# A scheduler's queue model learns that GpSimd sums delay queued VectorE work, and side work waits for GpSimd's queue

## The chip, the cores and the metric

One core of one Trainium2 chip. The metric is the device time of one launch in microseconds; lower is better. The engines are TensorE (PE, its weight loads PEld), VectorE (DVE), ScalarE (ACT), GpSimd (POOL) and SyncE (SP, which issues the DMAs).

## What is computed

One layer of a hybrid decoder for a prompt of 512 tokens and 8 sample tokens that share all weights. Everything is float32 at the interface. Cut to what matters:

```python
h = rms_norm(x, g); z = h @ w_in                      # (520, 2048) @ (2048, 7168)
y = [ silu(gate_pool) * Pool(u) |                     # trailing means over 2/4/8/16 positions
      silu(gate_dil)  * DilAttn(q, k, v) |            # 3 groups of 4 heads, QK-norm, merged by denominators
      silu(gate_mem)  * MemAttn(q_mem, mem) ]         # 4 heads over 256 memory tokens, QK-norm
x = x + y @ w_out                                     # (520, 1536) @ (1536, 2048)
```

The memory keys and values come from `rms_norm(mem) @ w_mem_kv` (2048 x 1024). The sample tokens attend to cached windows, and the shifted caches are outputs too.

## The kernel before

All activations are kept transposed (128 channels on the partitions, 520 tokens along the free axis). Every weight block of 128 x 512 is loaded by a DMA (`wraw`), and split in two float32r parts, `whi` by ScalarE (L167) and `wlo` by VectorE (L177); activations are split as `xh`, `xl` in the same way. A product is then three matmuls (xh·whi, xl·whi, xh·wlo), each over two halves of 260 tokens. The function `emit_split` makes one split and issues the next load; `whi` and `wlo` have 6 buffers each (SPB). I count the splits from 0, in the order in which VectorE makes them: 16 for the first four blocks (0 to 15), 12 for the next three z blocks (16 to 27), then the stage that mixes four z blocks with the eight blocks of `w_mem` (the memory stage, splits 28 to 75: a memory block's split feeds 12 matmuls of 256 columns, a z block's 24 of 260), then the other z blocks, then the 16 output blocks.

Between the matmuls of this main stream, side tasks run as Python generators: the norm of each q and k (`norm_task`: Square, a sum over partitions on GpSimd by `p_ar` at L210, `rsqrt_steps`, then a product), the sample tokens' scores and values (`sample_scores`, `sample_values`), the attentions and the pool branch (`pool_task`). A task takes one step when it is advanced. What is issued when is decided while the program is built, by the class `Clock`: it keeps an estimated time for each engine (`free`), for TensorE (`pe`) and for each tile (`written`, `used`). The order so made is the program: every engine runs its instructions in that order.

```python
def busy():
    return ck.backlog("dve") > 2.5 or ck.backlog("act") > 2.5
def tick():
    budget = ck.pe + 1.2
    for task in list(tasks):
        if task[0] > ck.pe: continue
        if ck.pe > budget or busy(): break
        if not advance(task): tasks.remove(task)
```

`tick` is called after every six main matmuls. `task[0]` is the estimated time at which the task's last step ends, plus 1 us. `backlog(eng)` is `free[eng] - pe`. `p_ar` calls `Clock.hold(s, e)`: VectorE instructions that the model places in that stretch are put behind it, and if VectorE's queue already reaches beyond `s`, its `free` time is moved by `e - s`. At the end of the z stage the output blocks begin (`need_split`): before the matmuls that read a slot of y (12 slots in the order YORDER, the last one of the pool branch's group 0) the tasks are pushed until that slot is there.

Of the kernel before, what the change touches and what calls it, by code (L numbers as in the profile page):

```python
# [48 lines left out]
class Clock:  # L49
# [5 lines left out]
    def __init__(self):  # L55
        self.pe = 0.0
        self.free = {"act": 0.0, "dve": 0.0, "pool": 0.0, "sp": 0.0, "hbm": 0.0}
        self.last = 0.0
        self.written = {}
        self.used = {}  # L60
        self.held = []

    def after(self, ins, outs):
        t = 0.0
        for a in ins:
            t = max(t, self.written.get(a.tensor.name, 0.0))
        for a in outs:
            t = max(t, self.used.get(a.tensor.name, 0.0))
        return t
# [11 lines left out]
    def use(self, eng, dur, ins, outs, shared=True):  # L81
        if eng == "pe":
            dep = max([self.written.get(a.tensor.name, 0.0) for a in ins])
            self.pe = max(self.pe, dep) + dur
            end = self.pe
            for a in ins:
                n = a.tensor.name
                self.used[n] = max(self.used.get(n, 0.0), end)
            for a in outs:
                n = a.tensor.name  # L90
                self.written[n] = max(self.written.get(n, 0.0), end + self.LAT)
                self.used[n] = max(self.used.get(n, 0.0), end)
            self.last = max(self.last, end + self.LAT)
            return
        start = max(self.free[eng], self.after(ins, outs))
        if eng == "dve" and shared and not any(a.tensor.name.startswith("ps") for a in ins):
            for s, e in self.held:
                if s <= start < e:
                    start = e
        end = start + dur  # L100
        self.free[eng] = end
        self.done(end + self.LAT, ins, outs)

    def hold(self, s, e):

        if s < self.free["dve"]:
            self.free["dve"] += e - s
        self.held = [h for h in self.held if h[1] > self.pe] + [(s, e)]

    def dma(self, nbytes, ins, outs):  # L110
# [17 lines left out]
def trunk(ctx, tc, nc, I, O):  # L128
    ck = Clock()
# [117 lines left out]
        return True  # L247

    def busy():
        return ck.backlog("dve") > 2.5 or ck.backlog("act") > 2.5  # L250

    def tick():
        budget = ck.pe + 1.2
        for task in list(tasks):
            if task[0] > ck.pe:
                continue
            if ck.pe > budget or busy():
                break
            if not advance(task):
                tasks.remove(task)  # L260
# [792 lines left out]
    for g, (w, d) in enumerate(WINS):  # L1053
        a, n, e = D2D[g]
# [290 lines left out]
```

## Time and profile before

| | us |
|---|---|
| median of 3 runs (894.66 to 895.25) | 895.0 |
| the profiled execution | 894.77 |
| its span | 893.0 |
| PE busy | 884.6 (99%) |
| PEld busy | 873.5 |
| DVE busy | 647.2 (72%) |
| ACT busy | 388.4 (43%) |
| POOL busy | 286.8 (32%) |

The granted TensorE clock is 1.00 over the span. 1.8 us of the profiled execution lie outside its span. A busy time is the sum of the instructions' own times; an instruction that is held up while it runs counts as busy for that time too.

### The profile page before, as it was taken

What the parts mean: (1) busy time and instruction counts of PE and PEld (TensorE: products, weight loads), DVE (VectorE), ACT (ScalarE), POOL (GpSimd) and SP (SyncE); (2) the same over time, 40 slices, a digit from 0 to 9 for tenths busy, and PEclk for the clock granted to TensorE, in tenths of its full rate; (3) what the DMA queues carried; (4) which work ended last, traced back from release to release, by engine and by line L of the source; (5) the groups of instructions that cost most, each with busy time, mean ns of one, the idle gap of its engine ahead of it and who ended that gap; (6) DMA issues with size and microseconds to landing.
All of it is one profiled execution on the core that took longest, in us unless ns stands there. A gap on an engine that the chain in (4) does not pass through costs nothing.

```text
span 893.0 us, 18390 instructions
## 1 busy us (share of the span) xinstructions
PE 884.6 (99%) x7226; PEld 873.5 (98%) x7226; DVE 647.2 (72%) x1226; ACT 388.4 (43%) x796; POOL 286.8 (32%) x96
## 2 busy tenths in 40 slices
PE   9999999999999999999999999999999999999998
PEld 8999999999999999999999999999999999999998
DVE  6788899965487869988798886888769679422321
ACT  7665565534436434544335343345433615222220
POOL 0133364613346345533155522363334400000000
PEclk9999999999999999999999999999999999999999
DMA  9535346589977867677878799689887777799421
GB/s 325 196 128 184 129 162 197 172 265 315 332 256 246 277 212 233 240 267 257 302 229 304 221 335 338 216 306 313 287 277 259 285 255 242 261 409 330 145 79 49
DMA packets 84663, 219.57 MB, mean 246 GB/s; under 512 B 10712, under 2 KB 25176, under 8 KB 82392
## 3 DMA queue, kind: packets, MB, share of 16 engines
q1 hardware_dynamic: 84432, 218.13, 71.8%
q8 instruction: 56, 0.92, 0.4%
q14 instruction: 31, 0.25, 0.1%
q10 hardware_dynamic: 144, 0.26, 0.1%
HBM read 200.32 MB, written 106.25 MB: 343 GB/s over the span
## 4 chain that ended last, share of the span: by engine, by line
PE 93%; DVE 4%; issue 1%; DMA 1%; SPq 0%; ACT 0%; DVEq 0%
PE psm L220 81%; PE psb L220 12%; DVE wlo L177 1%; DVE sv L200 1%; PE psb L226 1%; DMA vn<-xT 0%; DVE sq L181 0%; DVE sk L177 0%; DVE tmp L181 0%; DMA o_mem<-vt 0%; DVE vt L177 0%; DVE qk L177 0%; DVE smx L196 0%; DVE tmp L177 0%; SPq L230 0%
## 5 line engine op out<-in xcount | busy, mean ns | idle before, releaser
L220 PE MATMUL psm<-xh,whi 128*128 128x260 f32 x2088 | 431.5, 287 | 1.6 <-ACT whi L167 0.7
L220 PE MATMUL psm<-xh,wlo 128*128 128x260 f32 x2088 | 422.9, 283 | 2.4 <-DVE wlo L177 2.3
L220 PE MATMUL psm<-xl,whi 128*128 128x260 f32 x2088 | 421.9, 283 | 0.0
L220 PEld LDWEIGHTS psm<-xh,whi 128*128 128x128 f32 x2088 | 323.8, 189 | 8.4 <-issue 5.5
L220 PEld LDWEIGHTS psm<-xh,wlo 128*128 128x128 f32 x2088 | 322.6, 188 | 3.2 <-DVE wlo L177 3.2
L220 PEld LDWEIGHTS psm<-xl,whi 128*128 128x128 f32 x2088 | 322.2, 188 | 0.0
L177 DVE TENSOR_TENSOR wlo<-wraw,whi 128x512 fp32r<-128x512 f32 x304 | 248.6, 838 | 47.9 <-ACT whi L167 47.8
L167 ACT ACTIVATE whi<-wraw 128x512 fp32r<-128x512 f32 x304 | 180.0, 621 | 169.2 <-PE psm L220 137.9
L210 POOL PARTITION_ALL_REDUCE sk<-sk x32 | 131.0, 4094 | 175.6 <-DVE sk L177 128.8
L210 POOL PARTITION_ALL_REDUCE sq<-sq x32 | 102.7, 3213 | 128.3 <-ACT sq L167 128.3
L177 DVE TENSOR_TENSOR tmp<-psm,vn 128x260 f32<-128x260 f32 x30 | 11.5, 424 | 89.5 <-PE psm L220 79.3
L167 ACT ACTIVATE sk<-sk,smx 128x256 f32<-128x256 f32 (+1 forms) x64 | 35.4, 553 | 71.0 <-DVE smx L187 37.0
L210 POOL PARTITION_ALL_REDUCE mx<-mx x17 | 46.6, 2739 | 55.0 <-DVE mx L177 55.0
L167 ACT ACTIVATE tmp<-tmp 128x520 f32<-128x520 f32 (+2 forms) x76 | 46.3, 610 | 33.8 <-DVE sq L181 28.7
L167 ACT ACTIVATE sq<-qk 128x520 f32<-128x520 f32 x28 | 17.8, 634 | 71.9 <-DVE qk L177 63.6
L220 PE MATMUL psb<-y,whi 128*128 128x256 f32 x192 | 41.3, 282 | 0.0
L177 DVE TENSOR_TENSOR qk<-psm,rsx 128x260 f32<-128x260 f32 x56 | 21.2, 420 | 22.7 <-PE psm L220 22.7
L220 PE MATMUL psb<-y,wlo 128*128 128x256 f32 x128 | 35.9, 281 | 0.0
L167 ACT ACTIVATE tmp<-sq,eps 128x520 f32<-128x520 f32 (+1 forms) x32 | 22.2, 695 | 28.2 <-POOL sq L210 27.8
L220 PEld LDWEIGHTS psb<-y,whi 128*128 128x128 f32 x192 | 31.6, 188 | 0.0
L200 DVE CUSTOM_DVE_ANT_1 sv<-sv,sk,sy 128x384 f32<-128x384 f32 x32 | 31.1, 1009 | 0.6
L181 DVE SCALAR_TENSOR_TENSOR qk<-qk,gains_r,sq 128x520 f32<-128x520 f32 x28 | 27.7, 989 | 1.0
(131 smaller groups left out, 742.3 us busy)
## 6 DMA issues: line engine op xcount, KB each, us to landing
o_cache<-cache SPq DMA_DIRECT2D x88, 712.0 KB, 7.3
wraw<-w_in SPq DMA_DIRECT2D x208, 256.0 KB, 5.3
o_cache<-cache SPq DMA_DIRECT2D x24, 584.0 KB, 6.3
wraw<-w_out SPq DMA_DIRECT2D x48, 256.0 KB, 4.9
wraw<-w_mem SPq DMA_DIRECT2D x32, 256.0 KB, 3.9
vn<-xT SPq DMA_DIRECT2D x31, 260.0 KB, 5.3
o_zero<-zero SPq DMA_DIRECT2D x6, 1024.0 KB, 7.3
sk<-dks SPq DMA_DIRECT2D x16, 384.0 KB, 5.4
```

The source lines that it names most:

```text
L167: nc.scalar.activation(out=out, in_=in_, func=func, scale=scale, bias=bias, **kw)
L177: nc.vector.tensor_tensor(out=out, in0=in0, in1=in1, op=op)
L181: nc.vector.scalar_tensor_tensor(out=out, in0=in0, scalar=scalar, in1=in1, op0=op0, op1=op1)
L200: nc.vector.tensor_tensor_reduce(out=out, in0=in0, in1=in1, scale=1.0, scalar=init, op0=op0, op1=op1, accum_out=accum)
L210: nc.gpsimd.partition_all_reduce(t, t, P, op)
L220: nc.tensor.matmul(out, lhsT=lhsT, rhs=rhs, start=start, stop=stop)
L226: nc.tensor.transpose(out, in_, ident)
```

## The change

The model's class keeps a list `recent` of the tiles that VectorE's queued instructions write, with their estimated ends. When a sum on GpSimd holds VectorE from `s` to `e`, the tiles in `recent` that end later than `s + 0.7` are now taken to be written and free `e - s` later; before, only the engine's `free` time was moved. And `busy()`, which keeps `tick` from beginning steps of side tasks, is now true as well when GpSimd's estimated queue is more than 1.0 us ahead of TensorE. No instruction is added or removed; their order changes on every engine.

```diff
@@ class Clock
+        self.recent = []
@@ use(): after an instruction of any engine but TensorE
         end = start + dur
         self.free[eng] = end
         self.done(end + self.LAT, ins, outs)
+        if eng == "dve":
+            self.recent = [r for r in self.recent if r[1] > self.pe] + [(a.tensor.name, end) for a in outs]
 
     def hold(self, s, e):
 
         if s < self.free["dve"]:
             self.free["dve"] += e - s
+            late = [(n, t) for n, t in self.recent if t > s + 0.7]
+            self.recent = [r for r in self.recent if r not in late] + [(n, t + e - s) for n, t in late]
+            for n, t in late:
+                self.written[n] = max(self.written[n], t + e - s + self.LAT)
+                self.used[n] = max(self.used[n], t + e - s + self.LAT)
         self.held = [h for h in self.held if h[1] > self.pe] + [(s, e)]
@@ trunk()
     def busy():
-        return ck.backlog("dve") > 2.5 or ck.backlog("act") > 2.5
+        return ck.backlog("dve") > 2.5 or ck.backlog("act") > 2.5 or ck.backlog("pool") > 1.0
```

In the rows that follow, source lines of the change are 8 higher than those of before (L185 is the former L177, L175 the former L167, L228 the former L220).

VectorE in the memory stage, from the `wlo` of split 43 to that of split 46 (`smx`, `sk` are the sample tokens' scores, `tmp`, `sq`, `qk` the end of a norm). Before:

```order
L177 TENSOR_TENSOR wlo_1631<-wraw_1368,whi_1630 128x512
L177 TENSOR_TENSOR wlo_1651<-wraw_1402,whi_1650 128x512
L177 TENSOR_TENSOR wlo_1669<-wraw_1423,whi_1668 128x512
L192 COPY qms_83<-qk_795 128x8
L192 COPY cs_84<-vt_1553 128x8
L177 TENSOR_TENSOR wlo_1707<-wraw_1446,whi_1706 128x512
```

In the change:

```order
L185 TENSOR_TENSOR wlo_1648<-wraw_1368,whi_1647 128x512
L185 TENSOR_TENSOR wlo_1668<-wraw_1409,whi_1667 128x512
L185 TENSOR_TENSOR wlo_1687<-wraw_1428,whi_1686 128x512
L204 TENSOR_REDUCE smx_1698<-sk_984 128x2
L195 TENSOR_SCALAR smx_1698<-smx_1698 128x2
L185 TENSOR_TENSOR sk_1637<-sk_1637,qms_83 128x512
L189 SCALAR_TENSOR_TENSOR tmp_1704<-sq_1594,tmp_1704 128x520
L189 SCALAR_TENSOR_TENSOR sq_1594<-tmp_1704,tmp_1703 128x520
L189 SCALAR_TENSOR_TENSOR qk_995<-qk_995,gains_r_66,sq_1594 128x520
L185 TENSOR_TENSOR wlo_1737<-wraw_1446,whi_1736 128x512
```

Two copies of 8 elements stood between the splits 45 and 46; now a score's maximum, the next score's product and the end of a norm stand there.

ScalarE a little earlier, from the `whi` of split 33 to that of split 35 (`tmp` with `eps`, `tmp`, `tmp` are the three steps of a reciprocal root, `sq` with `qk` the Square of the next norm). Before:

```order
L167 ACTIVATE whi_1364<-wraw_1020 128x512
L167 ACTIVATE sq_1383<-qk_795 128x520
L167 ACTIVATE whi_1398<-wraw_1067 128x512
L167 ACTIVATE whi_1419<-wraw_1105 128x512
L167 ACTIVATE tmp_1435<-sq_1262,eps_67 128x520
L167 ACTIVATE tmp_1434<-tmp_1435 128x520
```

In the change:

```order
L175 ACTIVATE whi_1364<-wraw_1020 128x512
L175 ACTIVATE tmp_1381<-sq_1262,eps_67 128x520
L175 ACTIVATE tmp_1380<-tmp_1381 128x520
L175 ACTIVATE tmp_1381<-tmp_1380 128x520
L175 ACTIVATE sq_1397<-qk_795 128x520
L175 ACTIVATE whi_1405<-wraw_1067 128x512
L175 ACTIVATE whi_1424<-wraw_1105 128x512
```

The reciprocal root's three steps and the Square now stand ahead of the `whi` of splits 34 and 35.

TensorE at the beginning of the output blocks, around the last of the pool branch's four products (`vt`, `kmem`, which here holds `pool_w`); `xh_35` is the slot that this product's result ends in, by VectorE's y, ScalarE's `xh_35` and VectorE's `xl_51`. Before:

```order
L220 MATMUL psb_9939<-vt_9872,kmem_625_3700 128x260
L220 MATMUL psb_9940<-vt_9872,kmem_625_3700 128x260
L220 MATMUL psm_9793<-xh_32_95,whi_9853 128x260 x2
L220 MATMUL psm_9793<-xl_48_111,whi_9853 128x260 x2
L220 MATMUL psm_9793<-xh_32_95,wlo_9854 128x260 x2
L220 MATMUL psm_9793<-xh_33_96,whi_9853 128x260 x2
L220 MATMUL psm_9793<-xl_49_112,whi_9853 128x260 x2
L220 MATMUL psm_9793<-xh_33_96,wlo_9854 128x260 x2
L220 MATMUL psm_9793<-xh_34_97,whi_9853 128x260 x2
L220 MATMUL psm_9793<-xl_50_113,whi_9853 128x260 x2
L220 MATMUL psm_9793<-xh_34_97,wlo_9854 128x260 x2
L220 MATMUL psm_9793<-xh_35_98,whi_9853 128x260 x2
```

In the change:

```order
L228 MATMUL psm_9771<-xh_34_97,wlo_9850 128x260 x2
L228 MATMUL psb_9957<-vt_9909,kmem_629_3691 128x260
L228 MATMUL psb_9958<-vt_9909,kmem_629_3691 128x260
L228 MATMUL psm_9771<-xh_35_98,whi_9849 128x260 x2
L228 MATMUL psm_9771<-xl_51_114,whi_9849 128x260 x2
```

The product stood 18 main matmuls ahead of the first reader of its slot; now it stands directly ahead of it.

## Rows read from the trace of the kernel before

**Rows 1.** The page: busy time of the engines.

```profile
PE 884.6 (99%) x7226; PEld 873.5 (98%) x7226; DVE 647.2 (72%) x1226; ACT 388.4 (43%) x796; POOL 286.8 (32%) x96
```

**Rows 2.** TensorE's waits: who, us in total, times, longest.

```profile
PE psm L220 <- DVE wlo L177: 2.3, 3, 1.2
PE psm L220 <- ACT whi L167: 0.7, 1, 0.7
```

**Rows 3.** Windows: stretch and length, then PE, PEld, DVE, ACT, POOL busy, clock, DMA.

```profile
93.60:121.50 27.90, 26.71 (x225) 26.51 (x223) 24.73 (x37) 16.72 (x33) 14.26 (x4) 1.00 0.40 132
121.50:154.30 32.80, 32.80 (x278) 32.80 (x277) 29.86 (x60) 19.66 (x43) 12.69 (x5) 1.00 0.61 197
154.30:181.00 26.70, 25.70 (x217) 25.49 (x216) 25.16 (x47) 15.89 (x37) 14.51 (x6) 1.00 0.60 188
```

**Rows 4.** Timeline of ACT, 92 to 100 us: start, length, instruction, idle before.

```profile
92.59 0.62 ACT L167 ACTIVATE whi<-wraw 128x512 fp32r<-128x512 f32 x1
...
93.64 1.14 ACT L167 ACTIVATE whi<-wraw 128x512 fp32r<-128x512 f32 x2
...
97.97 1.31 ACT L167 ACTIVATE tmp<-tmp 128x520 f32<-128x520 f32 x2 [2.58 <-DVE mx L181]
```

**Rows 5.** Timeline of DVE, 92 to 100 us.

```profile
92.43 1.89 DVE L177 TENSOR_TENSOR wlo<-wraw,whi 128x512 fp32r<-128x512 f32 x3
...
97.00 0.41 DVE L181 SCALAR_TENSOR_TENSOR tmp<-mx,tmp 128x256 f32<-128x256 f32 x1
97.45 0.43 DVE L181 SCALAR_TENSOR_TENSOR mx<-tmp,tmp 128x256 f32<-128x256 f32 x1
```

**Rows 6.** Timeline of PE: the matmul that reads split 34's wlo first.

```profile
99.02 0.40 PE L220 MATMUL psm<-xh,wlo 128*128 128x260 f32 x2
```

**Rows 7.** Timeline of DVE, 107 to 133 us.

```profile
109.46 0.68 DVE L177 TENSOR_TENSOR sk<-sk,qms 128x512 f32<-128x512 f32 x1
...
111.00 2.40 DVE L181 SCALAR_TENSOR_TENSOR tmp<-sq,tmp 128x520 f32<-128x520 f32 x1
...
114.17 2.65 DVE L181 SCALAR_TENSOR_TENSOR qk<-qk,gains_r,sq 128x520 f32<-128x520 f32 x1
...
120.78 0.68 DVE L177 TENSOR_TENSOR wlo<-wraw,whi 128x512 fp32r<-128x512 f32 x1
121.39 0.15 DVE L206 RECIPROCAL sz<-sz 128x2 f32<-128x2 f32 x1
...
122.36 1.29 DVE L177 TENSOR_TENSOR wlo<-wraw,whi 128x512 fp32r<-128x512 f32 x2
...
124.50 0.68 DVE L196 TENSOR_REDUCE smx<-sk 128x2 f32<-128x512 f32 x1
...
125.29 0.69 DVE L181 SCALAR_TENSOR_TENSOR tmp<-sq,tmp 128x520 f32<-128x520 f32 x1
...
127.43 1.28 DVE L177 TENSOR_TENSOR wlo<-wraw,whi 128x512 fp32r<-128x512 f32 x2
```

**Rows 8.** Timeline of POOL, 92 to 130 us.

```profile
110.24 3.60 POOL L210 PARTITION_ALL_REDUCE sk<-sk  x1 [12.78 <-DVE sk L177]
113.74 3.53 POOL L210 PARTITION_ALL_REDUCE sq<-sq  x1
```

**Rows 9.** Timeline of PE: the first readers of the wlo of splits 43, 46, 50.

```profile
117.48 0.51 PE L220 MATMUL psm<-xh,wlo 128*128 128x260 f32 x2 [1.19 <-DVE wlo L177]
...
123.28 0.40 PE L220 MATMUL psm<-xh,wlo 128*128 128x260 f32 x2
...
131.59 0.28 PE L220 MATMUL psb<-y,wlo 128*128 128x256 f32 x1
```

**Rows 10.** Timeline of PE: the last product of the pool branch.

```profile
760.74 1.04 PE L220 MATMUL psb<-vt,kmem 128*128 128x260 f32 x4
```

**Rows 11.** Timeline of ACT: the slot of y that waits for that product.

```profile
762.34 0.64 ACT L167 ACTIVATE xh<-y 128x520 fp32r<-128x520 f32 x1 [3.60 <-DVE y L181]
```

**Rows 12.** Timeline of DVE: the slot's second part.

```profile
763.01 0.70 DVE L177 TENSOR_TENSOR xl<-y,xh 128x520 fp32r<-128x520 f32 x1 [0.71 <-ACT xh L167]
```

## The prediction

> **What bounds the kernel now.** I read the page first. TensorE is busy for 884.6 of the span's 893.0 us, at the full granted clock [rows 1, 3], and the change adds and removes no matmul. So a better order can give back at most what TensorE loses in waits. TensorE's own waits come next: three waits for a `wlo` make 2.3 us, and one for a `whi`, at the program's first product, 0.7 us [rows 2]. The kernel can thus become at most some 2.3 us faster by a better order, and as much slower as a worse order makes splits late. Third, the windows of the stretch where those waits lie, the memory stage: VectorE is busy for 24.73 of 27.90, 29.86 of 32.80 and 25.16 of 26.70 us there [rows 3]. It has only 3.2, 2.9 and 1.5 us of air in these three pieces, and every `wlo` stands in its queue. In this stage the order on VectorE decides; later VectorE has more air. Last, the program's order before and in the change, at the places shown with the change.
>
> What a sum on GpSimd costs VectorE is in two pairs of rows. The sum of 110.24 found `tmp` begun at 111.00, which took 2.40 us, where the same instruction takes 0.69 us elsewhere: 1.7 us more. The sum of 113.74 found `qk` begun at 114.17, which ended at 116.82, 3.1 us after the sum's begin, where the triple `tmp`, `sq`, `qk` otherwise takes 2.14 us in all (125.29 to 127.43), so that `qk` lost about 1.9 us [rows 7, 8]. An instruction caught in a sum comes free about 2.2 to 2.5 us after the sum's begin. I price a sum that catches VectorE's queue at 1.7 to 1.9 us.
>
> **The change, part by part.**
>
> *The model's new lines themselves* cost nothing at run time: they act while the program is built. All that counts is the order.
>
> *Place 1, splits 34 and 35 on ScalarE.* Before, `whi` of 34 and 35 stood ahead of a reciprocal root; they ran at 93.64, and the root's second step then waited 2.58 us for VectorE's `mx`, harmlessly [rows 4]. In the change the root and a Square stand ahead of them. I walk it: VectorE's three `wlo` end their slots at 94.24 (three of 0.60 from 92.43), `tmp` and `mx` follow (0.41 and 0.43 with 0.04 between), so `mx` is there at 95.1 [rows 5]. ScalarE's two steps then take 1.31 [rows 4], the Square 0.6, `whi` of split 34 another 0.6: 97.6. The Square releases a sum on GpSimd at about 97.1, which catches the `wlo` of split 34 and lets it end at about 99.9 (97.1, 2.2 and 0.6). TensorE wanted it at 99.02 [rows 6]. That is a new wait of 0.9 us.
>
> *Place 2, split 46.* Ahead of its `wlo`, counted from where the orders part, VectorE has in the change one norm triple (2.14), one maximum with its scaling (0.79, 124.50 to 125.29), one score product (0.60) and one set of the sample's values (0.97, 121.39 to 122.36) more than before, and nothing less: 4.5 us [rows 7]. The score product that comes forward releases one sum more, too: with 1.9 it is 6.4 us. Before, that `wlo` ended at 121.46 and TensorE read it at 123.28 [rows 7, 9], a lead of 1.8. If VectorE idles as much as before, TensorE gets there 4.6 us later than before; if all 3.2 us of air of this stretch [rows 3] were filled, 1.4 us later. Place 1 leaves VectorE waiting from about 95.5 to 97.6, some 2.1 us of air that isn't filled, so at most 1.1 us is won: 3.5 to 4.6. I take 4.0. In this number place 1's wait is contained, and also that the old wait of 1.19 us at split 43 [rows 9] goes.
>
> *Place 3, split 50.* From split 49 to 50 a set of values and a triple now stand (0.97 and 2.14) where a maximum and a triple stood (0.79 and 2.14), and a norm's Square ahead on ScalarE makes a sum fall in. Extra 0.2 and 1.9; the lead there is about 1.7: before, the `wlo` ended at 128.1 (127.43 and 0.68) and was read at 131.59, a lead of 3.5 [rows 7, 9], of which the 1.8 of split 46 are used up. That leaves 0.4, and 1.2 if VectorE also waits for buffers that the late TensorE frees late. I take 1.0, bounds 0 and 1.9.
>
> *The rest of the memory stage, splits 51 to 75.* By split 76 the order has one half-width triple more ahead than at place 2, some 1.3 us (its steps take 0.41 and 0.43 [rows 5]). The last two pieces have 2.9 and 1.5 us of air [rows 3], already used by an order that had leads of 2 to 4 us. I price further short waits at 1.5 us together. Below, the old wait late in the stage (2.3 less the 1.19 of split 43 leaves at most 1.1 us [rows 2, 9]) could go without a new one, -1.1; above, two more places like place 2 without air, +4.
>
> *The later z blocks.* TensorE loses hardly anything to a split there before [rows 2], and by split 128 the same instructions stand ahead of it in both orders. I take nothing.
>
> *The first output block.* The last product of the pool branch stands directly ahead of the matmul that reads its result. Before, 18 matmuls of 0.12 us, 2.2 us, lay between. The chain from the product's begin: 760.74 to the end of `xh` at 762.98 and of `xl` at 763.71 [rows 10 to 12], while TensorE has issued the product's four passes about 0.7 us after its begin (1.04 less the last one's flight), at 761.45. With nothing between, TensorE waits 1.5 us for `xh`, does two matmuls (0.24) and waits 0.45 us more for `xl`: 2.0 us. Bounds: 1.5, if other splits of the slot's neighbours aren't in the way, and 2.4, if a `whi` or a `wlo` stands ahead on ScalarE or VectorE. DMA queues: the loads and stores follow the splits and tasks and bring the same bytes; I cost their moves at nothing, since the loads run 10 buffers ahead.
>
> **Sum.** 4.0 + 1.0 + 1.5 + 2.0 = 8.5 us. On the profiled execution's 894.77 (893.0 of span and 1.8 around it) this is 903.3; the median of the runs is 0.2 higher, so **903.5 us**, 0.9% slower. Low ends together: 1.4 + 0 - 1.1 + 1.5 = 1.8, or 896.8. High ends: 4.6 + 1.9 + 4 + 2.4 = 12.9, or 907.9. About 0.2% (1.8 us) is what a measurement of this kernel can tell from no change.
>
> **Rivals.**
>
> *The model is right and the order fits the chip better (faster).* Then the three waits for a `wlo` go without new ones, and nothing is lost at the output blocks: 2.3 us less [rows 2], 892.7. For it: the order before met sums that came later than planned. Against it: place 1 and place 2 can be counted, and the product at the output block stands where it stands. It decides at split 46: if its `wlo` is there by TensorE's need, this is the case. 6%.
>
> *VectorE's air takes most of it.* Place 2 comes to 1.4, places 3 and the rest to 0, the output block to 2.0: 3.2 us, 898.2. For it: in the stretch to 121.5 VectorE did idle 3.2 us. Against it: place 1 puts 2.1 us of idling in the same stretch. 22%, from 897 to 900.
>
> *It stays the same*, because the gains at the old waits (2.3) pay for place 2 at its low end and the output block: 895 to 896. 6%.
>
> *TensorE's clock falls.* The granted clock stayed at 1.00 in every stretch of rows 3, with waits of at most 1.2 us in them; the new wait at split 46 would be some 3 us. If the clock fell to the lower of its two levels, each microsecond of matmuls after it would take two until it rose, and 6 to 8 us of such a stretch give 3 to 4 more: about 907. The Trainium skill ("TensorE: Matmul & The Clock Gate", Part 1, "What's actually happening") says that the throttled clock is the default and that activity releases it; no run here shows what gap ends that. 5%.
>
> **How the numbers follow.** The forecast with its neighbourhood (900 to 907) has 61%, and these four 39%. Slower by over 0.2% are the forecast, the second rival and the last: 0.88. Within 0.2%: 0.06. Faster: 0.06. The range leaves out the faster case, the unchanged one and the last: **897.5 to 907.0**.
>
> **What would show it.** Right: a wait of TensorE for `wlo` of about 1 us near 100 us and one of 3 to 4 us near 127 us, further ones of about 1 us before 185 us, and near 771 us TensorE waiting 1.5 us for `xh` and 0.4 for `xl`; the wait of 1.19 at 117 gone; DVE's busy share of the memory stage nearly the same over a longer stretch. Wrong in the first step: no wait at 100. Wrong in the main step: split 46's `wlo` ahead of TensorE's need, or no extra sum on GpSimd before it. The output block is independent of both: if the whole is slower by only about 2 us, the memory stage was misjudged.

## The result and the profile after

| | before | after |
|---|---|---|
| median, us | 894.97 (894.66 to 895.25) | 905.46 (904.9 to 907.17) |
| span of the profiled execution, us | 893.0 | 905.4 |

The change makes the kernel 1.2% slower: the ratio is 1.0121, with an interval of 1.0109 to 1.0133. The forecast of 903.5 us was 2.0 us too low, and the range (897.5 to 907.0) holds the result. The profiled execution of the changed kernel took 907.17 us, 1.7 us more than its median. Its mean granted clock is 0.998, as in the execution of 905.93 us; the two of 905.0 and 904.9 us have 1.000. So part of what stands in this trace, told below, is not in every execution.

The page of the changed kernel, its busy line. TensorE's busy time has risen by 4.7 us and VectorE's by 21.8 us, with the same number of instructions [rows 1]: both count an instruction as busy while it runs slowly or is held.

```profile
PE 889.3 (98%) x7226; PEld 876.0 (97%) x7226; DVE 669.0 (74%) x1226; ACT 387.0 (43%) x796; POOL 287.2 (32%) x96
```

TensorE's waits in the changed kernel (who, us in total, times, longest). Three waits for a `wlo` with 2.3 us [rows 2] have become eight with 8.3 us, 7.7 us of them in the memory stage; the waits for `xh` and `xl` at the first output block are new.

```profile
PE psm L228 <- DVE wlo L185: 4.4, 5, 1.6
PE psb L228 <- DVE wlo L185: 3.9, 3, 1.7
PE psm L228 <- ACT xh L175: 1.2, 1, 1.2
PE psm L228 <- ACT whi L175: 1.2, 2, 0.7
PE psm L228 <- DVE xl L185: 0.2, 1, 0.2
```

The windows of the memory stage, of the changed kernel (stretch and length, then PE, PEld, DVE, ACT, POOL busy, clock, DMA):

```profile
93.60:128.00 34.40, 30.66 (x253) 30.04 (x252) 30.06 (x46) 18.84 (x41) 17.06 (x5) 1.00 0.43 142
128.00:163.00 35.00, 31.99 (x260) 30.99 (x260) 31.42 (x61) 17.50 (x39) 17.08 (x6) 1.00 0.51 165
163.00:193.00 30.00, 28.28 (x224) 28.02 (x224) 26.12 (x52) 16.87 (x38) 11.70 (x4) 0.94 0.65 209
```

The same three stretches of the kernel before:

```profile
93.60:128.00 34.40, 33.21 (x279) 33.01 (x278) 31.09 (x51) 20.47 (x41) 14.26 (x4) 1.00 0.48 158
128.00:163.00 35.00, 35.00 (x297) 35.00 (x296) 32.09 (x64) 21.22 (x47) 17.12 (x7) 1.00 0.59 191
163.00:193.00 30.00, 29.00 (x242) 28.79 (x241) 26.76 (x49) 16.07 (x37) 13.31 (x5) 1.00 0.61 189
```

By the records TensorE does 26, 37 and 18 matmuls fewer in the three stretches, and VectorE, on which the `wlo` stand, is not fuller but a little emptier: it idles 4.3, 3.6 and 3.9 us where it idled 3.3, 2.9 and 3.2. TensorE waits for VectorE at one split, and VectorE then waits for what comes late: behind split 46 it idles 2.33 us for a `whi` (at 128.44 below).

The timeline of PE in the changed kernel: the matmuls behind the long waits. By the splits that they read they are 34 (99.88), 43 (118.92), 46 (126.17), 50 (136.44), 57 (150.96), the `whi` of 61 (158.81) and 69 (178.00); then the first output block.

```profile
99.88 0.51 PE L228 MATMUL psm<-xh,wlo 128*128 128x260 f32 x2 [0.85 <-DVE wlo L185]
...
118.92 0.51 PE L228 MATMUL psm<-xh,wlo 128*128 128x260 f32 x2 [1.64 <-DVE wlo L185]
...
126.17 0.51 PE L228 MATMUL psm<-xh,wlo 128*128 128x260 f32 x2 [1.24 <-DVE wlo L185]
...
136.44 0.39 PE L228 MATMUL psb<-y,wlo 128*128 128x256 f32 x1 [0.80 <-DVE wlo L185]
...
150.96 0.38 PE L228 MATMUL psb<-y,wlo 128*128 128x256 f32 x1 [1.41 <-DVE wlo L185]
...
158.81 0.51 PE L228 MATMUL psm<-xh,whi 128*128 128x260 f32 x2 [0.70 <-ACT whi L175]
...
178.00 0.39 PE L228 MATMUL psb<-y,wlo 128*128 128x256 f32 x1 [1.72 <-DVE wlo L185]
...
772.33 1.04 PE L228 MATMUL psb<-vt,kmem 128*128 128x260 f32 x4
774.62 0.51 PE L228 MATMUL psm<-xh,whi 128*128 128x260 f32 x2 [1.25 <-ACT xh L175]
775.36 0.51 PE L228 MATMUL psm<-xl,whi 128*128 128x260 f32 x2 [0.23 <-DVE xl L185]
```

Each wait costs some 0.27 us more than the idle time in its row. Some 0.16 us of it is that the row counts from the end of the matmul before (0.28 us after its start), while matmuls otherwise follow each other every 0.12 us; 0.11 us is that the pair behind the wait takes 0.51 us where a pair otherwise takes 0.40.

The timeline of DVE in the changed kernel, the instructions ahead of those splits; the `wlo` of 34, 43, 46 and 50 are at 97.46, 118.18, 125.44 and 135.70.

```profile
94.55 0.42 DVE L189 SCALAR_TENSOR_TENSOR mx<-tmp,tmp 128x256 f32<-128x256 f32 x1
...
97.46 3.57 DVE L185 TENSOR_TENSOR wlo<-wraw,whi 128x512 fp32r<-128x512 f32 x3 [2.08 <-ACT whi L175]
...
110.11 2.06 DVE L185 TENSOR_TENSOR wlo<-wraw,whi 128x512 fp32r<-128x512 f32 x1
...
112.77 2.24 DVE L200 COPY qms<-qk 128x8 f32<-128x8 f32 x1
...
116.12 2.14 DVE L185 TENSOR_TENSOR ysm<-sy,sz 128x2 f32<-128x2 f32 x1
118.18 1.88 DVE L185 TENSOR_TENSOR wlo<-wraw,whi 128x512 fp32r<-128x512 f32 x3
...
122.10 2.62 DVE L189 SCALAR_TENSOR_TENSOR sq<-tmp,tmp 128x520 f32<-128x520 f32 x1
...
125.44 0.68 DVE L185 TENSOR_TENSOR wlo<-wraw,whi 128x512 fp32r<-128x512 f32 x1
128.44 1.29 DVE L185 TENSOR_TENSOR wlo<-wraw,whi 128x512 fp32r<-128x512 f32 x2 [2.33 <-ACT whi L175]
...
131.46 2.11 DVE L185 TENSOR_TENSOR ysm<-sy,sz 128x2 f32<-128x2 f32 x1
```

The timeline of POOL in the changed kernel, the sums that held VectorE there:

```profile
97.00 3.28 POOL L218 PARTITION_ALL_REDUCE sq<-sq  x1 [4.98 <-ACT sq L175]
109.01 3.60 POOL L218 PARTITION_ALL_REDUCE sk<-sk  x1 [8.73 <-DVE sk L185]
112.52 6.73 POOL L218 PARTITION_ALL_REDUCE sq<-sq  x2
121.61 3.55 POOL L218 PARTITION_ALL_REDUCE sk<-sk  x1 [2.37 <-DVE sk L185]
131.12 3.44 POOL L218 PARTITION_ALL_REDUCE sq<-sq  x1 [5.96 <-ACT sq L175]
```

And TensorE's clock. Windows of the changed kernel behind the wait that ended at 178.00 (columns as above):

```profile
178.00:179.00 1.00, 1.00 (x6) 1.00 (x7) 0.93 (x3) 0.00 (x0) 0.33 (x1) 0.73 0.85 326
179.00:181.00 2.00, 2.00 (x11) 2.00 (x10) 2.00 (x4) 0.00 (x0) 0.00 (x0) 0.50 0.78 202
```

The granted clock was 0.50, the lower of its two levels, for about 3.3 us from 178.5 to 181.8. Matmuls took twice as long there, which would be 1.7 us; what it cost, by a kernel with the same order and no such fall, is 1.1 us (shown in the part on the prediction).

### The profile page after: what moved, and what is told of

The parts are those of the page before. It is cut to its first block, busy times and chain, and to the rows that moved or that the text cites. A ratio compares the mean times of both kernels' runs of the same rounds, so it can differ in the third digit from the quotient of the medians.

```text
span 905.4 us, 18392 instructions
## 1 busy us (share of the span) xinstructions
PE 889.3 (98%) x7226; PEld 876.0 (97%) x7226; DVE 669.0 (74%) x1226; ACT 387.0 (43%) x796; POOL 287.2 (32%) x96
## 4 chain that ended last, share of the span: by engine, by line
PE 88%; DVE 6%; issue 2%; ACT 2%; DMA 1%; SPq 0%; ACTq 0%; DVEq 0%
PE psm L228 79%; PE psb L228 9%; DVE wlo L185 2%; DVE sq L189 1%; DVE tmp L189 1%; DVE sv L208 1%; ACT whi L175 1%; DMA vn<-xT 1%; ACT tmp L175 1%; PE psb L234 1%; DMA wraw<-w_mem 0%; DMA wraw<-w_in 0%; DVE sk L185 0%; DVE ysm L185 0%; DVE qms L200 0%
## 5 line engine op out<-in xcount | busy, mean ns | idle before, releaser
L228 PE MATMUL psm<-xh,whi 128*128 128x260 f32 x2088 | 431.7, 287 | 3.2 <-ACT xh L175 1.2
L228 PE MATMUL psm<-xh,wlo 128*128 128x260 f32 x2088 | 423.6, 283 | 4.5 <-DVE wlo L185 4.4
L228 PE MATMUL psm<-xl,whi 128*128 128x260 f32 x2088 | 422.4, 283 | 0.2 <-DVE xl L185 0.2
L228 PEld LDWEIGHTS psm<-xh,whi 128*128 128x128 f32 x2088 | 324.0, 189 | 10.5 <-issue 6.2
L228 PEld LDWEIGHTS psm<-xh,wlo 128*128 128x128 f32 x2088 | 322.8, 189 | 5.9 <-DVE wlo L185 5.9
L228 PEld LDWEIGHTS psm<-xl,whi 128*128 128x128 f32 x2088 | 322.6, 188 | 0.4 <-DVE xl L185 0.4
L185 DVE TENSOR_TENSOR wlo<-wraw,whi 128x512 fp32r<-128x512 f32 x304 | 257.1, 864 | 60.7 <-ACT whi L175 60.4
L175 ACT ACTIVATE whi<-wraw 128x512 fp32r<-128x512 f32 x304 | 178.5, 620 | 141.8 <-PE psm L228 125.8
L175 ACT ACTIVATE sk<-sk,smx 128x256 f32<-128x256 f32 (+1 forms) x64 | 35.5, 555 | 102.9 <-DVE smx L195 55.6
L185 DVE TENSOR_TENSOR tmp<-psm,vn 128x260 f32<-128x260 f32 x30 | 11.6, 424 | 90.5 <-PE psm L228 79.0
L175 ACT ACTIVATE tmp<-tmp 128x520 f32<-128x520 f32 (+2 forms) x76 | 46.4, 610 | 27.2 <-DVE sq L189 23.5
L175 ACT ACTIVATE sq<-qk 128x520 f32<-128x520 f32 x28 | 17.8, 634 | 57.0 <-DVE qk L185 55.9
L228 PE MATMUL psb<-y,whi 128*128 128x256 f32 x192 | 41.4, 282 | 0.0
L228 PE MATMUL psb<-y,wlo 128*128 128x256 f32 x128 | 36.8, 287 | 4.0 <-DVE wlo L185 3.9
L175 ACT ACTIVATE tmp<-sq,eps 128x520 f32<-128x520 f32 (+1 forms) x32 | 22.2, 695 | 34.2 <-POOL sq L218 27.1
L185 DVE TENSOR_TENSOR qk<-psm,rsx 128x260 f32<-128x260 f32 x56 | 21.3, 421 | 18.0 <-PE psm L228 18.0
L228 PEld LDWEIGHTS psb<-y,whi 128*128 128x128 f32 x192 | 31.9, 189 | 0.0
L189 DVE SCALAR_TENSOR_TENSOR tmp<-sq,tmp 128x520 f32<-128x520 f32 (+1 forms) x32 | 26.8, 838 | 4.9 <-ACT tmp L175 4.9
L228 PEld LDWEIGHTS psb<-y,wlo 128*128 128x128 f32 x128 | 24.4, 191 | 4.8 <-DVE wlo L185 4.8
(131 smaller groups left out, 765.0 us busy)
```

The costliest lines, as they stand in the source:

```text
L175: nc.scalar.activation(out=out, in_=in_, func=func, scale=scale, bias=bias, **kw)
L185: nc.vector.tensor_tensor(out=out, in0=in0, in1=in1, op=op)
L189: nc.vector.scalar_tensor_tensor(out=out, in0=in0, scalar=scalar, in1=in1, op0=op0, op1=op1)
L228: nc.tensor.matmul(out, lhsT=lhsT, rhs=rhs, start=start, stop=stop)
```

## The experiments

**The theories.** In the builder's model a `wlo` that is marked late is late for everyone who reads it, and its reader is TensorE: `use("pe")` begins a matmul at `max(self.pe, dep)`, so `ck.pe` jumps. But `ck.pe` is also the clock by which `tick` decides that a task is due (`task[0] <= ck.pe`) and by which `backlog` reads a queue (`free - pe`). *Theory A* says that this is what costs time: the model's TensorE waits in thought, so it lets more side work begin per main matmul, and that work then makes the real TensorE wait. *Theory B*: the late times re-order the chains through VectorE's, ScalarE's and GpSimd's tiles, and TensorE's time in the model has no part. *Theory C*: GpSimd's term in `busy()` puts side work off, and it comes in a bunch.

**The parts of the change apart.** The late rule alone is the change without its last line:

```diff
-        return ck.backlog("dve") > 2.5 or ck.backlog("act") > 2.5 or ck.backlog("pool") > 1.0
+        return ck.backlog("dve") > 2.5 or ck.backlog("act") > 2.5
```

> The late rule alone; the old busy(), without GpSimd's term. Theory A (the lateness of wlo tiles enters the time that the queue model keeps for TensorE; that time runs ahead, tasks fall due sooner and backlogs read smaller, so more side work is begun per main matmul): the waits for wlo in the memory stage stay as in the changed kernel, 8 to 10 us of them, and the time is 903 to 907 us, 1.009 to 1.013 of before. Theory B (the late rule re-orders the side chains through the tiles of VectorE and ScalarE alone; TensorE's model time has no part): the same here, 903 to 907. Theory C (GpSimd's term in busy() puts work off, which then comes in a bunch): without that term the waits go, 894 to 897 us.

Measured: 906.14 us (905.71 to 908.05), ratio 1.0129 (1.0113 to 1.0144). The term alone is the kernel before with that line added the other way:

> GpSimd's term in busy() alone; tiles queued on VectorE keep their old times when a sum is begun. Theories A and B: the memory stage is as before, one wait of about 1.2 us for wlo near 117 us, and the time is 893.5 to 896 us. Theory C: the waits of the changed kernel return, 902 us or more.

Measured: 894.94 us, ratio 0.9999 (0.9989 to 1.0008). Theory C falls: GpSimd's term is worth nothing that can be measured, and the late rule has the whole loss.

**Who sees the late times.** The third kernel keeps a second time for each tile, without the lateness, and lets TensorE's model time read that one:

```diff
         if eng == "pe":
-            dep = max([self.written.get(a.tensor.name, 0.0) for a in ins])
+            dep = max([self.plain.get(a.tensor.name, 0.0) for a in ins])
```

(`plain` is set wherever `written` is, except in `hold`.)

> Both rules, but the model's time of TensorE is advanced with tile times that hold no lateness; VectorE, ScalarE and GpSimd still see the late times. Theory A: the memory stage's waits fall back to about 1.5 us for wlo, as before, and TensorE's granted clock stays at 1.00 near 180 us; the wait of the first output block (about 2 us near 762 us) may stay, since there the chain of side work itself is later: 895 to 899 us. Theory B: the memory stage's waits stay, 902 to 907 us.

Measured: 895.92 us (895.33 to 897.05), ratio 1.001 (1.0 to 1.0019). The fourth is its mirror image: `hold` writes the late time to a table `seen`, which TensorE's model time alone reads.

```diff
             for n, t in late:
-                self.written[n] = max(self.written[n], t + e - s + self.LAT)
-                self.used[n] = max(self.used[n], t + e - s + self.LAT)
+                self.seen[n] = max(self.seen.get(n, 0.0), self.written[n], t + e - s + self.LAT)
```

> Both rules, but only the model's time of TensorE sees the late times; the other engines' tiles keep the old ones. Theory A: the memory stage's waits appear as in the changed kernel (1.0 us near 100 us, 3 us between 118 and 127 us, 1 us near 136 us, more until 180 us), in all 7 to 10 us; the first output block may lose its wait; 899 to 905 us. Theory B: the memory stage is as before, 893 to 897 us.

Measured: 902.24 us (902.04 to 902.67), ratio 1.0081 (1.0066 to 1.0096). TensorE's waits in the third kernel and the one of its memory stage that is longer than 0.2 us, split 43's, as in the kernel before [rows 9]; then two of its three waits at the first output block (the third is 0.22 us for `xl`, at 762.77; of the 1.3 us for `xh` 0.53 are at the program's start):

```profile
PE psm L231 <- DVE wlo L188: 1.4, 2, 1.2
PE psm L231 <- ACT xh L178: 1.3, 2, 0.7
```

```profile
117.58 0.51 PE L231 MATMUL psm<-xh,wlo 128*128 128x260 f32 x2 [1.19 <-DVE wlo L188]
...
764.24 0.51 PE L231 MATMUL psm<-xh,whi 128*128 128x260 f32 x2 [0.72 <-ACT xh L178]
764.97 0.80 PE L231 MATMUL psm<-xl,whi 128*128 128x260 f32 x2 [0.23 <-DVE xl L188]
```

TensorE's waits in the fourth:

```profile
PE psm L229 <- DVE wlo L186: 6.0, 5, 2.0
PE psb L229 <- DVE wlo L186: 2.3, 3, 0.8
```

The two halves of the late rule cost 1.0 and 7.3 us, the whole change 10.5, so they don't simply add. But they part by place. With TensorE's model time left alone the memory stage's new waits are gone. With that time alone late there are 8.1 us of waits for a `wlo` in it (7.7 in the whole change): those at splits 34, 43, 46 and 50 are the same within 0.05 us, the later ones differ, and the first output block has none. Theory A holds for the memory stage, theory B does not. The orders say the same. This counts, in the programs, VectorE's instructions up to the `wlo` of a split:

| split | 34 | 43 | 46 | 50 | 57 | 69 | 74 | 76 |
|---|---|---|---|---|---|---|---|---|
| before | 118 | 144 | 149 | 165 | 186 | 229 | 244 | 252 |
| the change | 121 | 152 | 161 | 176 | 199 | 244 | 256 | 267 |
| late, not for TensorE | 118 | 144 | 149 | 165 | 186 | 229 | 244 | 255 |
| late for TensorE only | 121 | 152 | 161 | 176 | 199 | 247 | 259 | 268 |

With the late times kept from TensorE's time, VectorE's order up to split 74 is that of the kernel before; with them in it alone, it is that of the change up to split 50, and from split 46 on 11 to 18 instructions more stand ahead of a split than before. Whether the due times or the shorter backlogs bring more of them was not taken apart, nor what the later times of TensorE's own results in the model add.

**The first output block.** In the third kernel TensorE still waits there, 0.72 us for `xh` and 0.45 for `xl`, so this wait comes from the other half of the rule, or from the price of a chain. A maximum over partitions of 128x512 takes 1.78 us on GpSimd (at 301.27 in the trace before), a sum of the same size 3.23 us (at 313.32); the model charges both alike.

```diff
-        ck.use("pool", nfree(t) * 0.00563 + 0.35, [t], [t])
+        per = 0.00563 if op == RADD else 0.0028
+        ck.use("pool", nfree(t) * per + 0.35, [t], [t])
```

(`hold` uses `per` too.)

> The changed kernel, with the maximum over partitions priced in the queue model at half a sum's price, near what the trace of the changed kernel shows for it (1.78 us against 3.23 us for a sum of 128x512). There are no such maxima ahead of the memory stage's end that the planner would place otherwise. Theory A (the memory stage's waits come from TensorE's model time; the first output block's from a chain that the model plans late for another reason, its sums and maxima on GpSimd being charged as held time): the memory stage is as in the changed kernel, the wait of about 2 us at the first output block goes or moves: 902 to 904.5 us. Rival (that wait hangs on the memory stage's delay alone, which brings everything behind it): it stays, 904.5 to 907 us.

Measured: 904.6 us (904.1 to 905.09), ratio 1.0105 (1.0091 to 1.0119), 0.9 us below the change as it was timed before. By the time it lies a tenth outside theory A's bracket and within the rival's; the trace tells them apart. The memory stage's waits are the same within 0.03 us, that of 1.72 us at split 69 among them. No wait is left at the first output block, but a new one stands 43 us ahead of it:

```profile
730.71 0.51 PE L229 MATMUL psm<-xh,wlo 128*128 128x260 f32 x2 [1.15 <-DVE wlo L185]
```

So the output block's wait does not hang on the memory stage's delay, and of the 2.1 us won by its going some 1.4 were lost again. What it hangs on can be counted: between the pool branch's last product and the first reader of its slot lie no matmuls that write `psm` in the change and with the late rule alone (both wait 1.25 us for `xh`), 6 in the third kernel (0.72), 18 before and in the fourth, 30 with the maximum's price (no wait in these three). Where the last chain of side work falls decides, and small shifts of the model's times move it.

**One number of the planner.** If shifts move waits, then a due time does too. A task's delay of 1.0 us was changed in the kernel before, in the third kernel and in the whole change:

```diff
-        task[0] = ck.last + 1.0
+        task[0] = ck.last + 0.5
```

> The kernel before, with one number changed: a side task falls due 0.5 us after its last step in the model, where it was 1.0. If what costs time is side work that falls into a place where VectorE has no air, small shifts of the due times move it, and the two waits of before (1.3 us near 117 us, 1.2 us near 177 us) can go without a new one: 891 to 893.5 us. Rival: earlier due times bring more side work per main matmul as the late rule does, and waits appear in the memory stage: 896 to 904 us.

Measured: 893.68 us, ratio 0.9986 (0.9977 to 0.9995). The wait at 117 us is gone and another of 0.96 us stands at split 46, at 122.5 us; the one at 177 us is gone too, and one of 0.56 us stands at split 76, at 182.1 us. The time is a little above its bracket.

> As the kernel whose late times TensorE's model time does not see, with the delay of 0.5 us as well. Theory A: no wait for wlo over 0.5 us in the memory stage, and the output block without the wait it had: 891 to 893.5 us, the same as the kernel before with the delay of 0.5. Theory B (late marks re-order the chains through the other engines): 896 us or more.

Measured: 893.0 us, ratio 0.9979 (0.9969 to 0.9988). One wait, of 0.96 us, is longer than the 0.5 us that was expected, the time as expected.

> The whole change with the delay of 0.5 us. Theory A: the lateness still drives TensorE's model time ahead, so several waits of 0.7 to 1.9 us stand between 120 and 191 us, 7 to 9 us of them, whatever the delay: 899 to 905 us. Rival (the change only met the delay of 1.0 at a bad moment): with the other delay the waits go, 891 to 895 us.

Measured: 904.33 us (904.19 to 904.9), ratio 1.0103 (1.009 to 1.0117). The waits came otherwise than expected: two for a `wlo` in the memory stage, of 2.93 and 2.22 us, and one of 1.30 us for `vt` in place of several with 7 to 9 us; the granted clock was at its lower level for 10.2 us there. The loss is nearly that of the change (9.4 us for 10.5), though with the same delay and TensorE's time left alone (the kernel before this one) there is none. The rival falls, and theory A has its second pair of runs, 893.0 against 904.33 us. With TensorE's time left alone the late rule does no harm in the memory stage, but it gains nothing that can be told either: 893.0 us against 893.68 without the rule, 895.92 against 894.93 with the delay of 1.0.

**A version that beats both.** Two more settings of the kernel before. First the delay of 0.6 us with VectorE's limit in `busy()` lowered from 2.5 to 2.0:

> The kernel before with two numbers changed: the delay of a task 0.6 us for 1.0, and no side work while VectorE's queue is over 2.0 us ahead, for 2.5. If less work queued on VectorE ahead of a split brings its wlo earlier, the waits of before in the memory stage (1.3 and 1.2 us) go, and none comes back at the first output block: 890.5 to 893.5 us. Rival: work that is put off in the memory stage comes back in a later stage or at the first output block, with a wait of 1 to 3 us there, as the late rule's deferred chain did: 894 to 897 us.

Measured: 893.53 us, ratio 0.9992 (0.9983 to 1.0001): one wait of 1.7 us for a `wlo`, at 123.6 us, and none at the output block. It is at its bracket's edge, and the comparison can't tell it from the kernel before. Then the delay of 0.8 us alone:

> The kernel before with one number changed: the delay of a task 0.8 us for 1.0. If the gain of the delay of 0.5 is that due times differ a little and side work falls beside better splits by chance, this one differs from it by 1 to 3 us in some direction: 891 to 896 us. If a shorter delay is better as such, it lies between the two: 893.5 to 895 us.

Measured: 892.11 us (891.56 to 892.59), ratio 0.997 (0.9959 to 0.998). It doesn't lie between the times for 0.5 and 1.0 us, so a shorter delay is not better as such; it differs by 1.4 us, as the other branch has it, in which the settings differ by where the work falls. TensorE's waits in it:

```profile
PE psb L220 <- POOL zero L1065: 1.0, 1, 1.0
PE psm L220 <- DVE wlo L177: 0.9, 1, 0.9
PE psm L220 <- DVE tmp L177: 0.5, 1, 0.5
```

It is the fastest of all that ran, 0.3% faster than the kernel before and 1.5% than the change. TensorE's waits for a `wlo` fell from 2.3 to 0.9 us [rows 2]; the 2.3 are what the prediction had as the most that an order can give, and the 2.4 us gained are a little more, which fits a wait's costing more than its row shows.

## Why the prediction was right, and where its steps were off

The verdict, the mechanism (more VectorE work ahead of the splits of the memory stage, a product directly ahead of its reader) and the range were right. The forecast owes part of its closeness to luck: place 2 was taken too large and the rest of the stage too small. By its own steps:

*Place 1, split 34: right.* `mx` was forecast for 95.1 and its last step begins at 94.55 with 0.42 us; the sum was forecast for 97.1 and began at 97.00; the `wlo` was to end at 99.9, and TensorE read it at 99.88, against 99.02 before: 0.86 us, forecast 0.9.

*Place 2, split 46: right in kind, too large, and one of its statements false.* TensorE read that `wlo` at 126.17, 2.89 us later than before, where 4.0 was forecast (bounds 3.5 to 4.6, and 1.4 if all air were filled). The windows from the parting of the orders to the end of that `wlo`, before:

```profile
93.60:121.46 27.86, 26.67 (x224) 26.47 (x223) 24.69 (x36) 16.68 (x32) 14.26 (x4) 1.00 0.40 133
```

and in the change:

```profile
93.60:126.11 32.51, 28.84 (x238) 28.21 (x236) 30.05 (x46) 16.98 (x35) 17.06 (x5) 1.00 0.44 146
```

VectorE is busy 5.36 us longer (30.05 less 24.69), where I had 6.4: 4.5 of work and 1.9 for one more sum that catches it. It is the sum's term that failed: there is one more (POOL x5 for x4), but VectorE lost 0.9 us more by sums and not 1.9. One sum did cost about what I had: by their durations each of the five held one instruction 1.4 to 2.1 us longer than it takes elsewhere, 9.0 us together. But the four of before had cost 7.8 us, and two short copies caught with them some 0.7 more, against one and 0.4 now. So it was wrong to price the extra sum alone and to leave the others as they were. Of its air 0.7 us was filled (idle 2.46 for 3.17), close to the 0.6 that I took. 5.36 less 0.71, less the old lead of 1.8, is the 2.9 that was measured. "That the old wait of 1.19 us at split 43 goes" did not happen either: it grew to 1.64. I had counted the added work up to split 46 as one block. By the table above 8 of the 12 instructions stand ahead of split 43 already, where two sums in a row held a copy of 8 elements for 2.24 us and a product of 2 elements for 2.14 us. The delay at split 46 is thus made in three waits, not in one of 3 to 4 us near 127 as was said.

*Place 3, split 50: right.* 136.44 us against 131.59 before, 4.85 us. Some 0.5 us of it are four side matmuls that now stand ahead; the rest, 4.4 us, is 1.5 us more than at split 46, and the wait's own row has 0.80 us. Forecast was 1.0, with bounds of 0 and 1.9, and 5.0 for both places together. The sum that was to fall in is there: that of 131.12 held a product of 2 elements for 2.11 us (at 131.46).

*The rest of the memory stage: mis-sized.* The waits at splits 57, 61 and 69 idle 3.8 us, less the 1.0 us that the old wait near 177 us took; with what each costs beyond its row and with smaller stalls it is some 4.3 us, where I took 1.5 and had 4 as the upper bound. This is read from one matmul of a z block behind the stage, the 1015th that writes `psm` in each program: in the kernel before, in the change, and in the kernel with the maximum's price, whose order is that of the change on every engine until after 250 us and whose clock stays at 1.00.

```profile
201.38 0.48 PE L220 MATMUL psm<-xh,whi 128*128 128x260 f32 x2
```

```profile
211.14 0.40 PE L228 MATMUL psm<-xh,whi 128*128 128x260 f32 x2
```

```profile
209.97 0.40 PE L229 MATMUL psm<-xh,whi 128*128 128x260 f32 x2
```

It comes 9.76 us late in the change; 4.4 are there at split 50, and 1.1 are the clock's: the two kernels of the same order are 1.17 us apart here, and were 0.10 apart at split 69 (178.00 and 177.90).

*The first output block: right.* 1.25 us for `xh` and 0.23 for `xl`, and with the refilling of the pipeline 2.1 us; forecast 2.0.

*The later z blocks: right*, no new wait. Not foreseen were two waits in the second output block, at 788 and 789 us, which idle 0.73 us and cost some 1.05; the kernels with the late rule alone and with the maximum's price lack them, and what makes them was not followed.

*TensorE's clock, a rival of 5%, came on top, at a smaller price and not in every execution.* It cost the profiled execution 1.1 us, for 3.3 us at the lower level, where the rival had 3 to 4 us for 6 to 8. By the granted clock on record (0.998) the execution of 905.93 us lost about as much; the two at 1.000 did not. The forecast's sum and this loss were set as alternatives; they add.

In all, for the profiled execution: 2.9, 1.5, 4.3, 1.1 for the clock, 2.1 and 1.05 make 12.95 us; the later z blocks and the program's end give some 0.5 back, and 12.4 lie between the spans. Without the clock and the second output block it is some 10.3 us, and the two executions at the full clock are 10.0 longer than the median before. That they lack the second block's waits too would fit, but their traces were not taken.

The prediction took the order for given and explained only what it costs. Why the order is so, the runs add: of the change's two rules one does nothing that can be measured, and the other is right about VectorE (at place 1 the `wlo` does end so late) but is passed on to the clock by which the planner doles out side work.

## What to carry to other kernels

In a planner that fills a bound engine's time with side work, keep the time that says how far the main stream has come apart from estimates of waits: in this one, when a planned wait moved that clock, the plan asked for more work where it had already found too much. When judging a re-ordering, count the instructions ahead of each reader on the engine that has no air, at every reader and not only at the last one. And test a planner's numbers on the chip one by one: delays of 1.0, 0.8 and 0.5 us gave 1, 0.997 and 0.9986 of the time before, with no trend.

## What was not expected of the hardware

*The clock falls after a short gap, but not always.* The wait of 1.72 us at split 69 was followed by the lower level in the changed kernel. The same matmuls after the same wait ran at the full clock in the kernel with the maximum's price. Its windows:

```profile
178.00:179.00 1.00, 1.00 (x9) 1.00 (x10) 0.93 (x3) 0.00 (x0) 0.24 (x1) 1.00 0.82 303
179.00:181.00 2.00, 2.00 (x18) 1.82 (x17) 1.97 (x4) 0.00 (x0) 0.00 (x0) 1.00 0.70 199
```

In the whole change with the delay of 0.5 us it came with both waits of the memory stage, of 2.93 and 2.22 us: inside the first, which ended at 119.20, and behind the second, which ended at 141.70:

```profile
118.20:119.20 1.00, 0.00 (x0) 0.00 (x1) 1.00 (x2) 0.24 (x1) 1.00 (x1) 0.51 0.58 223
120.00:122.00 2.00, 2.00 (x12) 2.00 (x11) 1.97 (x5) 1.42 (x5) 0.09 (x1) 0.50 0.66 196
...
142.00:145.00 3.00, 3.00 (x17) 3.00 (x16) 3.00 (x7) 2.00 (x5) 1.37 (x1) 0.52 0.47 154
```

while one of 2.04 us, with TensorE's time alone late, was not followed by it. In the third kernel it came at 765.0, behind waits of only 0.22, 0.72 and 0.23 us; the pair at 764.97 above took 0.80 us. One kernel differs between executions too: of the eleven with the delay of 0.6 us (longest wait of the profiled one: 1.71 us), four have a granted clock of 0.998 and took 894.5 to 895.2 us, the others 0.999 or 1.000 and 893.1 to 893.9 us. So the length of the last gap alone doesn't say whether the clock falls. What it costs differs as well: 1.1 us for 3.3 us in the change; with the delay of 0.5 us the profiled execution, with 10.2 us at the lower level, was only 0.7 us longer than the one at 1.000 (904.9 and 904.19). That TensorE's waits for VectorE hide part of it there would fit, and was not followed.

*A sum on GpSimd holds tiny instructions as long as large ones.* The copy of 8 elements at 112.77 took 2.24 us, where such a copy takes 0.16 us undisturbed (at 95.22), and ended at 115.01, 2.5 us after the begin of the sum at 112.52; that sum and the one behind it take 6.73 us together, so by its record the first went on for about another microsecond (the profile's spans on GpSimd are rough). The Trainium skill ("SBUF — State Buffer", "Who interferes with whom") says that one of the two engines gets the shared pair of ports for its whole instruction and that the other blocks fully. The trace agrees that it blocks, and that a copy can be caught too, but VectorE came free before the sum's record ended.
